# A hybrid encoder on one core: where layer two's projections find their operands inside 256 bytes

## The chip, the core and the metric

The kernel runs on one core of one Trainium2 chip. The metric is the time of one execution on the device, in microseconds (us); the time before is a median of three runs. A stage of the kernel is named below by its stretch of the profiled execution, in us from the start of the span.

## The reference

Two layers of a bidirectional encoder trunk run over 272 positions (256 tokens and 16 meta tokens) of width 2048. Everything is float32. Cut to what matters here:

```python
def _layer(h, w_in, ..., w_out, ln1_w, ln1_b, w_ff1, w_ff2, ln2_w, ln2_b):
    proj = jnp.einsum('bld,dp->blp', h, w_in)          # 2048 -> 6176 columns
    gq, gk, gv, gr, glr, nq, nk, nv = jnp.split(proj, points, axis=-1)
    y_gla = _gla_mixer(gq, gk, gv, gr, glr, ...)       # gated linear attention, 4 heads
    y_na = _na_mixer(nq, nk, nv, na_rel_bias)          # neighbourhood attention, 16 heads
    mix = jnp.einsum('blm,md->bld', jnp.concatenate([y_gla, y_na], axis=-1), w_out)
    h = _layer_norm(DEEPNORM_ALPHA * h + mix, ln1_w, ln1_b)
    ff = jnp.einsum('blf,fd->bld', jnp.square(jax.nn.relu(jnp.einsum('bld,df->blf', h, w_ff1))), w_ff2)
    return _layer_norm(DEEPNORM_ALPHA * h + ff, ln2_w, ln2_b)
...
return h[:, N_META:]                                   # the meta tokens are dropped
```

## The kernel before

The residual stream lies transposed: 16 chunks of 128 features on the partitions, positions along the free axis. Each chunk is held as two parts of type fp32r, a high part (the value as the engine rounds it) and a low part (what is left). Weights come from memory in tiles `raw` of 128 x 1024 float32 (512 KB); ScalarE makes the high part `wh` of a tile (line 152) and VectorE the low part `wl` (line 153). A product is then three products, high by high, high weight by low part, low weight by high part. Which matmuls do them depends on the number of positions:

- `three`, with n of 272, 274 or 258 columns: three matmuls, at lines 165, 166 and 167. They stream the high part, the low part and the high part again. This is called a triple below. The two columns over 272 or 256 carry a gain and a bias of the norm through the product.
- `three`, with n = 256: a matmul of 512 columns at line 161 that streams both parts in one go, and one of 256 at line 162. This is called a pair below.
- `by_k`, where a stage starts on chunks that are still being made: matmuls one by one at line 191.

`by_m` calls `three` for 16 chunks in turn and 4 output tiles; a tile of weights serves 8 chunks. Between the tiles `pump` lets other work in: the attention heads' own matmuls (lines 505 to 540 and 597 to 653) with their steps on the other engines.

Where in SBUF an operand starts is set by two tables. Each table is indexed by a stage:

```python
ROOM = 640
WIDE = (23, 276), (3, 288), (20, T)        # chunk: start of the first part, step to the second, in elements
STARTS = (40, 48), (0, 8), (36, 4)         # weights: start of wh and of wl within their tiles
...
return self.parts(t, *WIDE[(2 if name != "x" else 1) if (self.l if late is None else late) else 0])
...
yield w[t], first.pop(0) if first else 1, l + (l and j > 11)    # which row of STARTS a tile of weights takes
```

A chunk's tile has 640 elements (2560 bytes) and a tile of weights 1088 (4352 bytes), both multiples of 256 bytes, and in the built program all of them start at 64 modulo 256. The columns of a weights tile that one matmul takes start at multiples of 512 bytes from the tile's start. So modulo 256 bytes all matmuls of a stage find their operands at the same places, four bytes to an element:

| stage | chunk's parts | weights `wh`, `wl` | matmuls |
|---|---|---|---|
| layer one | 156 and 236 | 224 and 0 | triples of 272, and of 274 in its first two feed-forward groups |
| layer two's projections (row 1 of both tables) | 76 and 204 | 64 and 96 | triples of 274 (K) and 272 (V, NA's k and v), `by_k` of 272 (V), pairs (q, gate, NA's q), whose 512 columns are 256 at 76 and 256 at 204 |
| layer two's first two feed-forward groups (row 1 of `WIDE`, row 2 of `STARTS`) | 76 and 204 | 208 and 80 | triples of 258 |
| the rest of layer two (row 2 of both) | both at 144, joined, so that 512 columns are contiguous | 208 and 80 | pairs, `by_k` of 256 |

`ln_add` writes layer two's chunks where row 1 of `WIDE` puts them. When the first norm of layer two is done, `renew` writes them once more at row 2.

The program is written out in a fixed order, each engine runs its own list, and only waits for operands tie the lists together.

Of the kernel before, what the change touches and what calls it, by code (L numbers as in the profile page):

```python
# [17 lines left out]
T = 256  # L18
# [18 lines left out]


ROOM = 640
WIDE = (23, 276), (3, 288), (20, T)  # L40
STARTS = (40, 48), (0, 8), (36, 4)


class Pair(tuple):
# [7 lines left out]
class Trunk:  # L52
# [88 lines left out]
    def made(self, ap, parts, l):  # L141
        if ap is None:
# [4 lines left out]
        wh, wl = (self.wp.tile([P, WB + 64], F32R, name=nm, tag=nm)[:, at:at + size]  # L147
                  for nm, at in zip(("wh", "wl"), STARTS[l]))
        for p in range(parts):
# [72 lines left out]
    def pair(self, pool, name, c, late=None):  # L222
        if name == "sp":
            return Pair(pool.tile([P, 2, L], F32R, name=f"{name}{c}", tag=f"{name}{c}", bufs=1))
        t = pool.tile([P, ROOM], F32R, name=f"{name}{c}", tag=f"{name}{c}", bufs=1)
        return self.parts(t, *WIDE[(2 if name != "x" else 1) if (self.l if late is None else late) else 0])

# [643 lines left out]
    def renew(self, end):  # L871
# [3 lines left out]
        for c in range(f["new"], end):  # L875
            while f["ready"] <= c:
                self.step(self.bg, 1)
            if n == T:
                self.x[c] = self.parts(self.x[c].tile, *WIDE[2])
            h, lo = self.x[c]  # L880
# [140 lines left out]
```

## Time and profile before

| | |
|---|---|
| median of 3 runs | 2371.94 us (2371.65 to 2372.04) |
| profiled execution | 2372.29 us, of which the span is 2370.1 us |
| granted TensorE clock, mean | 0.997 |
| TensorE matmul (PE) busy | 2337.7 us, 99% of the span, 17276 instructions |
| TensorE weight load (PEld) busy | 2223.8 us, 94% |
| VectorE (DVE), ScalarE (ACT), GpSimd (POOL) busy | 1576.1, 1188.2 and 283.5 us |
| layer two's projections | 1212.5 to 1557.9 us |
| layer two's first two feed-forward groups | 1650.0 to 1696.6 us |

Matmuls overlap, so that the duration of one (some 0.28 us for 272 columns) says little; what the stage pays for each is the time from one start to the next, and that is read from rows in order of time or from the number of matmuls in a stretch. In a stretch, a matmul that reaches in from before or is cut off at the end counts as well, so the count is some 2 too high.

### The profile page before, as it was taken

To read this page: it belongs to the slowest core of one execution; us is meant where nothing else is said; L and a number is where in the kernel's file an instruction comes from. 1 tells how busy PE (TensorE), PEld (TensorE's weight loads), DVE (VectorE), ACT (ScalarE), POOL (GpSimd) and SP (SyncE) were. 2 spreads that over 40 slices of the span, in tenths; PEclk is the share of its full clock that TensorE was granted. 3 is DMA by queue.
4 is the path that set the end of the run, shared out by engine and by line. 5 is a ranking of instruction groups with operands and counts; after the bars stand their busy time and mean duration, and the time that the engine had idled before them with its cause. 6 is when DMAs were issued, how large, how long until landed. Compare 5 with 4: busy or idle time off the path is not lost.

```text
span 2370.1 us, 43078 instructions
## 1 busy us (share of the span) xinstructions
PE 2337.7 (99%) x17276; PEld 2223.8 (94%) x17276; DVE 1576.1 (66%) x2473; ACT 1188.2 (50%) x1962; POOL 283.5 (12%) x447
## 2 busy tenths in 40 slices
PE   9999999999999999999999999999999999999997
PEld 9999999999999999999999899998988888888886
DVE  6688787785544455557577887778866555666655
ACT  6555555564433344444456555555654334444443
POOL 1164320020000000000020454300200000000000
PEclk9999999999999999999999999999999999999998
DMA  7544444555555555545545445446565555555553
GB/s 249 169 139 150 142 141 159 177 178 181 178 179 179 182 181 178 179 182 176 181 169 194 144 151 159 139 152 204 185 191 195 194 195 194 190 195 195 190 194 132
DMA packets 118359, 417.46 MB, mean 176 GB/s; under 512 B 13388, under 2 KB 16332, under 8 KB 118160
## 3 DMA queue, kind: packets, MB, share of 16 engines
q1 hardware_dynamic: 118160, 414.72, 53.1%
q8 instruction: 135, 2.21, 0.4%
q14 instruction: 64, 0.52, 0.1%
HBM read 412.57 MB, written 2.10 MB: 175 GB/s over the span
## 4 chain that ended last, share of the span: by engine, by line
PE 91%; DVE 4%; POOL 2%; issue 1%; ACT 1%; DMA 0%; SPq 0%; ACTq 0%; POOLq 0%; DVEq 0%
PE mm L161 21%; PE mm L165 16%; PE mm L166 16%; PE mm L167 16%; PE mm L162 11%; PE mm L191 6%; POOL lev L475 1%; PE bg L505 1%; DVE wl L153 1%; PE bg L648 1%; DVE acc L864 1%; PE bg L597 1%; DVE lev L481 0%; ACT wh L152 0%; ACT ns L580 0%
## 5 line engine op out<-in xcount | busy, mean ns | idle before, releaser
L153 DVE TENSOR_TENSOR wl<-raw,wh 128x1024 fp32r<-128x1024 f32 (+1 forms) x772 | 946.0, 1226 | 617.4 <-ACT wh L152 609.2
L152 ACT CAST wh<-raw 128x1024 fp32r<-128x1024 f32 (+1 forms) x772 | 804.3, 1042 | 901.8 <-PE mm L166 351.8
L165 PE MATMUL mm<-x,wh 128*128 128x272 f32 (+2 forms) x2176 | 623.3, 286 | 0.0
L166 PE MATMUL mm<-x,wh 128*128 128x272 f32 (+2 forms) x2176 | 617.7, 284 | 0.0
L167 PE MATMUL mm<-x,wl 128*128 128x272 f32 (+2 forms) x2176 | 616.7, 283 | 0.1
L165 PEld LDWEIGHTS mm<-x,wh 128*128 128x128 f32 x2176 | 407.7, 187 | 1.2 <-issue 0.4
L166 PEld LDWEIGHTS mm<-x,wh 128*128 128x128 f32 x2176 | 408.7, 188 | 0.0
L167 PEld LDWEIGHTS mm<-x,wl 128*128 128x128 f32 x2176 | 407.6, 187 | 0.5 <-DVE wl L153 0.5
L161 PE MATMUL mm<-x,wh 128*128 128x512 f32 x1152 | 398.0, 391 | 0.0
L162 PE MATMUL mm<-x,wl 128*128 128x256 f32 x1152 | 317.9, 276 | 0.2 <-DVE wl L153 0.2
L161 PEld LDWEIGHTS mm<-x,wh 128*128 128x128 f32 x1152 | 216.2, 188 | 45.3 <-issue 0.4
L161 PE MATMUL mm<-y,wh 128*128 128x512 f32 x704 | 241.6, 388 | 0.0
L162 PEld LDWEIGHTS mm<-x,wl 128*128 128x128 f32 x1152 | 216.2, 188 | 0.7 <-DVE wl L153 0.6
L166 PE MATMUL mm<-y,wh 128*128 128x272 f32 x704 | 199.2, 283 | 0.0
L165 PE MATMUL mm<-y,wh 128*128 128x272 f32 x704 | 199.2, 283 | 0.0
L167 PE MATMUL mm<-y,wl 128*128 128x272 f32 x704 | 198.9, 283 | 0.0
L162 PE MATMUL mm<-y,wl 128*128 128x256 f32 x704 | 193.5, 275 | 0.7 <-DVE wl L153 0.7
L161 PE MATMUL mm<-u,wh 128*128 128x512 f32 x512 | 175.6, 388 | 0.0
L475 POOL TENSOR_TENSOR lev<-be 128x128 f32<-128x128 f32 (+1 forms) x256 | 150.2, 617 | 115.2 <-PE bg L505 36.4
L161 PEld LDWEIGHTS mm<-y,wh 128*128 128x128 f32 x704 | 132.0, 188 | 27.0 <-ACT wh L152 0.2
L165 PE MATMUL mm<-u,wh 128*128 128x272 f32 x512 | 144.9, 283 | 0.0
L166 PE MATMUL mm<-u,wh 128*128 128x272 f32 x512 | 144.9, 283 | 0.0
(235 smaller groups left out, 3312.5 us busy)
## 6 DMA issues: line engine op xcount, KB each, us to landing
raw<-in_wff SPq DMA_DIRECT2D x512, 512.0 KB, 3.5
raw<-in_win SPq DMA_DIRECT2D x190, 512.0 KB, 3.5
raw<-in_wout SPq DMA_DIRECT2D x64, 512.0 KB, 3.6
nb<-in_nab SPq DMA_DIRECT2D x16, 352.0 KB, 3.8
out<-acc SPq DMA_DIRECT2D x8, 256.0 KB, 2.2
xraw<-in_xT SPq DMA_DIRECT2D x7, 272.0 KB, 5.4
wraw<-in_wup SPq DMA_DIRECT2D x2, 392.0 KB
raw<-in_win SPq DMA_DIRECT2D x4, 128.0 KB, 2.9
```

What stands on the lines that cost most here:

```text
L152: nc.scalar.copy(wh[:, c], raw[:, c])
L153: self.wl = nc.vector.tensor_tensor(wl[:, c], raw[:, c], wh[:, c].bitcast(F32), ALU.subtract).ins
L161: mm(ps, lhsT=wh[:, c:c + P], rhs=x.joined, start=first, stop=False)
L162: mm(ps[:, T:], lhsT=wl[:, c:c + P], rhs=xh[:, :T], start=False, stop=last)
L165: mm(o, lhsT=wh[:, c:c + P], rhs=xh[:, :n], start=first, stop=False)
L166: mm(o, lhsT=wh[:, c:c + P], rhs=xl[:, :n], start=False, stop=False)
L167: mm(o, lhsT=wl[:, c:c + P], rhs=xh[:, :n], start=False, stop=last)
L191: self.nc.tensor.matmul(ps[m][:, :n], lhsT=parts[p][0][:, c:c + P], rhs=acts[j][parts[p][1]][:, :n], start=j + p == 0, stop=j == nk - 1 an ...
L475: tt = lambda o, x, y: nc.gpsimd.tensor_tensor(o, x, y, ALU.subtract)
L505: nc.tensor.matmul(ps[:, b], lhsT=k[:, b], rhs=q[:, r], start=True, stop=True)
L597: nc.tensor.matmul(ps[hh][:, t * NKEY:t * NKEY + NKEY], lhsT=q[hs, NM + t * P:NM + t * P + P], rhs=k[hs, t, :], start=True, stop=True)
L648: nc.tensor.matmul(r[hs], lhsT=(v2 if rest else v1)[:, t, hs], rhs=p2[:, t, :] if rest else p1[:, 2 * t + hh, :], start=rest, stop=not rest)
```

## The change

One pair of numbers in each table. Layer two's chunks, as projections read them, start 8 elements into their tile with 300 elements from part to part, in place of 3 and 288: that is 96 and 16 modulo 256 bytes in place of 76 and 204. The weights of the projections start at elements 36 and 4, as those of the rest of layer two already do: 208 and 80 in place of 64 and 96. The triples of 258 in the first two feed-forward groups read the same chunks, so that their parts move too; their weights stay at 208 and 80.

```diff
 ROOM = 640
-WIDE = (23, 276), (3, 288), (20, T)
-STARTS = (40, 48), (0, 8), (36, 4)
+WIDE = (23, 276), (8, 300), (20, T)
+STARTS = (40, 48), (36, 4), (36, 4)
```

Every engine's list has the same instructions in the same order before and after, with the same waits; only addresses differ.

## The prediction

> **What bounds the kernel now.** First the page's busy times and the chain that ended last:
>
> ```profile
> PE 2337.7 (99%) x17276; PEld 2223.8 (94%) x17276; DVE 1576.1 (66%) x2473; ACT 1188.2 (50%) x1962; POOL 283.5 (12%) x447
> PE 91%; DVE 4%; POOL 2%; issue 1%; ACT 1%; DMA 0%; SPq 0%; ACTq 0%; POOLq 0%; DVEq 0%
> ```
>
> TensorE is busy all the time and carries 91% of the chain. Then the busy times by stretch, for the stages whose addresses change. The columns are the stretch, its length, and busy us with the instruction count for PE, PEld, DVE, ACT and POOL; then the granted clock, the DMA share and GB/s. The rows are layer two's projections as a whole, among them the gate's stretch, and the two feed-forward groups with 258 columns.
>
> ```profile
> 1212.50:1557.90 345.40, 339.15 (x2494) 315.23 (x2492) 277.89 (x489) 210.10 (x432) 130.12 (x205) 1.00 0.48 158
> 1315.90:1380.60 64.70, 61.36 (x371) 53.52 (x369) 58.30 (x94) 40.40 (x82) 41.64 (x70) 1.00 0.42 144
> 1650.00:1696.60 46.60, 46.60 (x391) 46.58 (x390) 43.54 (x76) 34.57 (x63) 13.12 (x8) 1.00 0.54 182
> ```
>
> PE idles 6.3 of 345.4 us in the projections, 3.3 of them in the gate's stretch, and not at all with 258 columns. The granted clock is 1.00. So a nanosecond per matmul, gained or lost, reaches the end nearly whole. The matmuls affected are counted from groups within the projections (the triples are also on lines 166 and 167, and the pairs' second matmul is on line 162):
>
> ```profile
> L161 PE MATMUL mm<-x,wh 128*128 128x512 f32 x320 | 115.0, 399 | 0.0
> L165 PE MATMUL mm<-x,wh 128*128 128x272 f32 x320 | 93.4, 292 | 0.0
> L167 PE MATMUL mm<-x,wl 128*128 128x274 f32 x64 | 18.5, 289 | 0.1
> L191 PE MATMUL mm<-x,wh 128*128 128x272 f32 x128 | 20.2, 287 | 0.1
> ```
>
> That is 320 pairs, 320 triples of 272, 64 triples of 274, and by the code 192 single matmuls at line 191 (these 128 and half as many on `wl`). To them come 2 x 64 = 128 triples of 258.
>
> **What a placement costs today.** Nothing is added or removed; the whole change is the time from one matmul's start to the next. The rows for that, by placement. First stretches of the same matmul throughout: layer one's triples of 272; line 191 on 272 in layer two; the pairs on contiguous parts.
>
> ```profile
> 600.00:1000.00 400.00, 400.00 (x3275) 400.00 (x3274) 203.40 (x225) 164.74 (x209) 0.00 (x0) 1.00 0.56 180
> 1244.50:1258.50 14.00, 14.00 (x115) 14.00 (x115) 11.27 (x19) 6.45 (x8) 0.90 (x2) 1.00 0.70 231
> 1740.00:2230.00 490.00, 490.00 (x2884) 433.83 (x2883) 294.24 (x377) 218.46 (x283) 0.00 (x0) 1.00 0.59 194
> ```
>
> Less the some 2 cut off at the edges (3 with the longer 512s) these are 122.2 ns a matmul, 124.2 ns, and 340.1 ns a pair. Then rows in order of time (start, duration, engine, line), the first and last of undisturbed series: 24 pairs, 11 triples of 272, 31 of 274, 64 of 258.
>
> ```profile
> 1263.09 0.39 PE L161 MATMUL mm<-x,wh 128*128 128x512 f32 x1
> ...
> 1271.07 0.39 PE L161 MATMUL mm<-x,wh 128*128 128x512 f32 x1
> ```
> ```profile
> 1532.29 0.28 PE L165 MATMUL mm<-x,wh 128*128 128x272 f32 x1
> ...
> 1535.99 0.28 PE L165 MATMUL mm<-x,wh 128*128 128x272 f32 x1
> ```
> ```profile
> 1219.00 0.29 PE L165 MATMUL mm<-x,wh 128*128 128x274 f32 x1
> ...
> 1230.21 0.28 PE L165 MATMUL mm<-x,wh 128*128 128x274 f32 x1
> ```
> ```profile
> 1656.26 0.28 PE L165 MATMUL mm<-x,wh 128*128 128x258 f32 x1
> ...
> 1678.94 0.28 PE L165 MATMUL mm<-x,wh 128*128 128x258 f32 x1
> ```
>
> Divided by 23, 10, 30 and 63: a pair takes 347.0 ns, a triple of 272 takes 370.0, of 274 takes 373.7, of 258 takes 360.0.
>
> Columns alone don't explain this: 272 against 258 is 5% more columns and 3% more time. What does fit is the number of 16-byte blocks (four columns) that a stream touches. The contiguous pair starts on a multiple of 16 (144) and touches 128 + 64 = 192 blocks: 340.1 / 192 = 1.771 ns a block. Layer one's parts start 12 bytes past a multiple of 16 (156, 236), so 272 columns touch 69 blocks: 122.2 / 69 = 1.771 ns. Two stages, the same quotient. I take it as the floor, and what a row has above it as its excess, in ns:
>
> - triple of 272 at 76/204, also 12 past: 3 x 69 blocks, floor 366.6, excess 3.4;
> - triple of 274: 3 x 70, floor 371.9, excess 1.8;
> - pair, two 256s and one more: 3 x 65, floor 345.3, excess 1.7;
> - line 191 on 272: floor 122.2, excess 2.0;
> - triple of 258: 3 x 66, floor 350.6, excess 9.4. These are split parts beside weights at 208 and 80, which is what the projections are to get;
> - contiguous parts beside weights at 208 and 80: excess 0.
>
> [...]
>
> **The change part by part.**
>
> *The chunk's parts.* 96 and 16 are multiples of 16, so each stream loses one block: 272 columns touch 68, 274 touch 69, 256 touch 64, 258 touch 65. The new floors are 361.3, 366.6, 340.0 (pair), 120.4 (line 191) and 345.3. Against today's times that is, with no excess left: 320 x 8.7 + 64 x 7.1 + 320 x 7.0 + 192 x 3.8 + 128 x 14.7 ns = 2.8 + 0.5 + 2.2 + 0.7 + 1.9 = 8.1 us less. That is the lower end.
>
> *The weights and how they meet the parts.* The excess at the new places isn't in the trace. Written as e ns for each triple or pair and e/3 for a single matmul, it adds (320 + 64 + 320 + 128 + 64) x e = 0.896 us for each ns of e. One bound is e = 0, the contiguous pairs' with the same weights. From the other side, the slowest series with these weights are a few pairs early in layer two's output projection:
>
> ```profile
> 1604.24 0.40 PE L161 MATMUL mm<-y,wh 128*128 128x512 f32 x1
> ...
> 1605.31 0.39 PE L161 MATMUL mm<-y,wh 128*128 128x512 f32 x1
> ...
> 1606.33 0.39 PE L161 MATMUL mm<-y,wh 128*128 128x512 f32 x1
> ```
>
> Three pairs take 357 ns each, within the rows' rounding of 10 ns in 1070, and the next three 340, at the same addresses: up to 17 above the floor, or some 8 a matmul. Between these ends I take e = 9.4, the excess of the 258s. It is the only row where these weights meet split parts. Then the sum is -8.1 + 0.896 x 9.4 = +0.3 us. By parts: triples of 272 go from 370.0 to 370.7 (+0.2 us), of 274 from 373.7 to 376.0 (+0.2), pairs from 347.0 to 349.4 (+0.8), line 191 from 124.2 to 123.5 (-0.1), and 258s from 360.0 to 354.7 (-0.7).
>
> *Making the weights.* A tile's two halves were made at three placements; here layer two's projections (64/96) and the rest of layer two (208/80), with count, busy us and mean ns:
>
> ```profile
> L153 DVE TENSOR_TENSOR wl<-raw,wh 128x1024 fp32r<-128x1024 f32 x16 | 19.6, 1224 | 11.0 <-ACT wh L152 10.8
> L152 ACT CAST wh<-raw 128x1024 fp32r<-128x1024 f32 x17 | 17.8, 1047 | 14.5 <-PE mm L166 7.9 <-DMA raw<-in_win 3.5 <-issue 1.3
> L153 DVE TENSOR_TENSOR wl<-raw,wh 128x1024 fp32r<-128x1024 f32 x181 | 221.8, 1225 | 183.6 <-ACT wh L152 181.7
> L152 ACT CAST wh<-raw 128x1024 fp32r<-128x1024 f32 x180 | 188.9, 1050 | 272.1 <-PE mm L161 165.2 <-issue 106.9
> ```
>
> 1224 and 1225 ns, 1047 and 1050: the writes don't feel the address. They also have cover, since a tile serves 8 x 347 ns = 2.8 us of pairs. If it were gone, 3 ns on each of some 100 tiles would be 0.3 us. I cost it, and the chunks' own writes, at nothing. Waits stay as they are.
>
> *Sum.* +0.3 us on the profiled execution's 2372.29 (span 2370.1 and 2.2 around it), which lies 0.35 above the median of the runs. On the median, that is 2372.3.
>
> **The rivals.**
>
> *Faster: the excess nearly vanishes.* For it: the contiguous pairs have none beside these very weights, and all new starts are multiples of 16. Against it: every split placement in layer two has some. The times today hint at where it would stop: 340.0, 346.7, 360.0, 366.7 and 373.3 are 51, 52, 54, 55 and 56 steps of 6.67 ns, and all rows but the 370.0 of the 272s lie on them. Were the new times the next step above their floors, the triples of 272 would go to 366.7 (-1.1 us), of 274 to 366.7 (-0.4), pairs to 340.0 (-2.2), 258s to 346.7 (-1.7) and line 191 to 122.2 (-0.4): -5.8 us, 2366.1. With no excess at all it is -8.1 us, 2363.8. [...]
>
> *Slower: parts and weights collide at every matmul.* The series at 357 ns shows that these weights can cost some 7 to 8 ns a matmul even beside parts on a multiple of 16. With 7: triples and pairs of 832 groups get 512 x 21 + 320 x 14 ns, line 191 gets 192 x 7, together 16.6 us, less the 8.1 of the blocks: +8.5 us, 2380.4. It decides from e = 14.4 on (+4.8 us). Against it: there the series was short and followed a disturbance; in the quiet stages after it, 340 holds. For it: in the projections the attention's own matmuls break in every few us, so series there seldom settle, and 76/204 beside 64/96 stays within 3.4 ns of its floor, which leaves more to lose than to win in the weights' part.
>
> *Hidden.* In the gate's stretch PE waits 3.3 us for the attention heads' steps, so a gain or loss on its 128 pairs (at most 0.9 us of the 8.1) could go into that wait. It changes no sign and gets no chance of its own.
>
> **How the numbers follow.** Excess like the 258s', within 4.7 us of now: 0.43. The collision: 0.32. The vanishing excess: 0.25. A measurement of this kernel tells 0.2% (4.7 us) from no change; the three cases fall one to each verdict, so faster 0.25, same 0.43, slower 0.32. The predicted time is the likeliest's, 2372.3. The range reaches to the stepped result of the faster rival and most of the way into the slower one: 2365.8 to 2379.0. The likeliest alone would lie between 2368 and 2376.
>
> **What would show it.** Starts in the changed kernel: pairs at 349 ns, triples of 272 at 371, of 274 at 376, of 258 at 355 if the sum is right. 340, 361 to 367, 367 and 345 to 347 are the faster rival; 354 and 382 the slower. Layer one's 122.2, the later pairs' 340.1 and the two halves' 1225 and 1050 ns must stand as they are; if the later pairs settle at another speed, upstream timing reaches past its stage and all of this is wrong.

## The result, and the profile after

The changed kernel takes 2375.24 us (median of 21 runs, 2373.89 to 2376.95) against 2371.94 before (21 runs, 2370.99 to 2372.92): 3.3 us more. The ratio is 1.0013, 95% interval 1.0007 to 1.0019. It is slower, clear of the interval, and within the 0.2% called no change. Its runs lie in two clusters, 2373.9 to 2374.8 (10 runs) and 2375.2 to 2377 (11), and the median is the lowest run of the upper one, so that its last half microsecond hangs on a run or two. The profiled execution (2373.98 us, span 2371.9) is of the lower one, so that its trace explains 1.7 to 2 us of the 3.3.

The stages that answer to those shown of before, each from its first matmul to its last: layer two's projections, the gate's stretch in them, and the two feed-forward groups of 258 columns. Columns as before.

```profile
1212.50:1559.70 347.20, 341.54 (x2494) 317.78 (x2492) 277.76 (x489) 210.20 (x432) 129.11 (x204) 1.00 0.51 157
1316.75:1381.50 64.75, 61.56 (x371) 53.53 (x369) 58.37 (x95) 40.41 (x82) 41.51 (x70) 1.00 0.46 145
1651.80:1698.50 46.70, 46.70 (x392) 46.70 (x391) 43.71 (x77) 34.73 (x63) 13.11 (x8) 1.00 0.61 182
```

The projections take 347.2 us in place of 345.4, the gate's stretch 64.8 in place of 64.7, and the 258s what they took. PE's busy time grew by more, 341.5 us against 339.2, and its idle time fell from 6.3 to 5.7 us: no new waits, but matmuls that follow each other more slowly, and waits that hide some of it. Series in order of time, first and last rows: 24 pairs, 32 triples of 274, 16 of 272, 7 of 272 that start 13 us after them, 54 of 258.

```profile
1263.52 0.40 PE L161 MATMUL mm<-x,wh 128*128 128x512 f32 x1
...
1271.49 0.40 PE L161 MATMUL mm<-x,wh 128*128 128x512 f32 x1
```
```profile
1219.12 0.29 PE L165 MATMUL mm<-x,wh 128*128 128x274 f32 x1
...
1231.00 0.29 PE L165 MATMUL mm<-x,wh 128*128 128x274 f32 x1
```
```profile
1299.84 0.29 PE L165 MATMUL mm<-x,wh 128*128 128x272 f32 x1
...
1305.53 0.29 PE L165 MATMUL mm<-x,wh 128*128 128x272 f32 x1
...
1312.97 0.28 PE L165 MATMUL mm<-x,wh 128*128 128x272 f32 x1
...
1315.17 0.28 PE L165 MATMUL mm<-x,wh 128*128 128x272 f32 x1
```
```profile
1662.73 0.28 PE L165 MATMUL mm<-x,wh 128*128 128x258 f32 x1
...
1681.81 0.28 PE L165 MATMUL mm<-x,wh 128*128 128x258 f32 x1
```

A pair takes 346.5 ns here (before 347.0), a triple of 274 takes 383.2 (373.7), a triple of 272 first 379.3 and then 366.7 at the same addresses (370.0), a triple of 258 still 360.0. Line 191's 272s, layer one's 272s and the later pairs, from stretches:

```profile
1245.00:1259.00 14.00, 14.00 (x114) 14.00 (x114) 10.89 (x17) 6.41 (x8) 0.89 (x2) 1.00 0.68 218
600.00:1000.00 400.00, 400.00 (x3275) 400.00 (x3274) 203.29 (x225) 164.63 (x209) 0.00 (x0) 1.00 0.59 181
1740.00:2230.00 490.00, 490.00 (x2883) 433.74 (x2882) 293.53 (x375) 217.83 (x282) 0.00 (x0) 1.00 0.64 194
```

Line 191 goes to some 125 ns (112 matmuls in 14 us); from start to start its undisturbed steps grew from 123.5 to 125.4 ns. What the change doesn't touch stands at 122.2 and 340.1.

### The profile page after: what moved, and what is told of

It reads as the page before. It is cut to its first block, busy times and chain, and to the rows that moved or that the text cites. A ratio compares the mean times of both kernels' runs of the same rounds, so it can differ in the third digit from the quotient of the medians.

```text
span 2371.9 us, 43078 instructions
## 1 busy us (share of the span) xinstructions
PE 2340.2 (99%) x17276; PEld 2226.9 (94%) x17276; DVE 1575.8 (66%) x2473; ACT 1187.7 (50%) x1962; POOL 282.0 (12%) x447
## 4 chain that ended last, share of the span: by engine, by line
PE 92%; DVE 3%; POOL 2%; issue 1%; ACT 1%; DMA 0%; SPq 0%; ACTq 0%; POOLq 0%; DVEq 0%
PE mm L161 22%; PE mm L165 16%; PE mm L166 16%; PE mm L167 16%; PE mm L162 11%; PE mm L191 6%; POOL lev L475 1%; PE bg L505 1%; DVE wl L153 1%; PE bg L648 1%; DVE acc L864 1%; PE bg L597 1%; DVE lev L481 0%; ACT wh L152 0%; PE bg L337 0%
```

## The experiments

Three theories were written down before the runs. A: the weights' new place costs, the parts' start on a multiple of 16 gains. B: the parts cost, whatever the weights. C: neither by itself, only how parts and weights meet. The expectations of the two halves and of the two places taken from a map name them so.

**One half of the change alone.** `e1_parts_only`:

```diff
-WIDE = (23, 276), (3, 288), (20, T)
+WIDE = (23, 276), (8, 300), (20, T)
```

> Only the parts move (96 and 16), the projections' weights stay at 64 and 96; 258s as in the changed kernel. Theory A, the weights' place at 208 and 80 makes the loss and the parts' starts on a multiple of 16 make a gain: faster than before, by 2 to 8 us (2364 to 2370), triples of 272 at 361 to 367 ns. Theory B, the loss comes from the parts alone, whatever the weights: like the changed kernel, 2374 to 2376, triples of 274 near 383 ns. Theory C, neither by itself but how the two meet: within 2 us of before, or anywhere; triples then differ from both kernels.

`e2_weights_only`:

```diff
-STARTS = (40, 48), (0, 8), (36, 4)
+STARTS = (40, 48), (36, 4), (36, 4)
```

> Only the projections' weights move (208 and 80), the parts stay at 76 and 204. Theory A: slower than the changed kernel's 2375, by the blocks that aren't saved, up to 2380; triples of 272 near 380 ns. Theory B: like before, 2371 to 2373, triples of 272 at 370 ns and of 274 at 374. Theory C: not the sum of the two halves of the change with e1.

The parts alone took 2374.73 us against 2371.91 (ratio 1.0012, 1.0003 to 1.0021), the weights alone 2374.29 (1.0009, 1.0000 to 1.0018). Each half costs 2.4 to 2.8 us and both together 3.3: by the medians they don't add up, though the intervals are wide, and A's gain isn't there. By kinds of matmul it is plainer. Means over all undisturbed series of each trace, worked out from the starts, in ns:

| kernel | parts, weights | 272 | 274 | pair | 258 |
|---|---|---|---|---|---|
| before | 76/204, 64/96 | 370.5 | 373.6 | 347.4 | 360.0 |
| parts alone | 96/16, 64/96 | 373.9 | 385.8 | 350.9 | 360.0 |
| weights alone | 76/204, 208/80 | 379.7 | 373.4 | 348.6 | 353.5 |
| changed | 96/16, 208/80 | 375.7 | 382.9 | 348.4 | 359.9 |

The new weights make the 272s dear beside the old parts (+9.2) and hardly dearer beside the new (+1.8). For 274s it is the parts that matter. A falls with the time of the parts alone, where it wanted a gain of 2 to 8 us, and B with the 272s of the weights alone, which it wanted at 370. C is what is left; its own expectation of the time (within 2 us, or anywhere) was too loose to be tested here. (The 258s of the weights-alone kernel have the very addresses of before's. More on them below.)

**The same distances at another place.** `e3_both_64_on` moves both by 64 bytes:

```diff
+WIDE = (23, 276), (24, 300), (20, T)
+STARTS = (40, 48), (52, 20), (36, 4)
```

> The changed kernel with the parts and the projections' weights both 64 bytes further (160 and 80; 272, that is 16, and 144), so that the distances stay. If only the distance of a stream from the weights counts, the projections' matmuls take what they take in the changed kernel (274s 383 ns, 272s 376, pairs 348) and the time is within 1 us of 2375, but for the 258s, whose weights don't move with them. If the place in 256 bytes itself counts, the triples change by several ns.

2375.0 us against 2371.91 (1.0012, 1.0003 to 1.0021), 272s 374.5, 274s 381.0, pairs 348.4: within 2 ns of the changed kernel for each. That agrees with a law of distances. It doesn't prove one, since series of this kind scatter by more than 2 ns (379.3 and 366.7 at the same addresses in the changed kernel).

**A map of quiet series.** `m1_map` computes nothing of the layers:

```python
for k in range(16):
    matmul(ps[:, :n], lhsT=w[wh + k % 8 * P], rhs=x[:, xh:xh + n])     # high by high
    matmul(ps[:, :n], lhsT=w[wh + k % 8 * P], rhs=x[:, xl:xl + n])
    matmul(ps[:, :n], lhsT=w[wl + k % 8 * P], rhs=x[:, xh:xh + n])     # or a pair in their place
```

> Nothing of the layers is computed: a kernel of matmul series alone, 149 placements, each with 16 triples or pairs on one PSUM bank, run in one order and then in the reverse one; starts are read from the trace. Blocks theory: with both parts at the same start a and weights at 208 and 80, a of 0, 16, 32, 48 take 3 x 1.77 = 5.3 ns less a triple of 272 than the other twelve starts, 361.3 against 366.6, if the excess is the same. Steps theory: all quiet series lie on multiples of 6.67 ns, so 366.7 for both. For the kernels' placements: before 370 (272), 374 (274), 347 (pair); after 376, 383, 348; a rival, that the differences come from the work around the series and not from the placement, gives the same time for both in these quiet series.

Without any surrounding work, the kernels' placements gave, in the two orders: before 369.9 and 370.0 (272s), 380.0 and 373.4 (274s); changed 366.6 and 376.6, 383.4 twice; weights alone 380.0 twice, 373.4 twice; parts alone 373.2 and 373.4, 386.6 twice. These are close to the kernels' own numbers. So the placement makes them, and the rival, that the surroundings alone do, falls. With both parts at one start a and weights at 208/80, 272s took 380.0, 375.8, 377.1 and 373.2 ns at a of 0, 16, 32 and 48, against 370.0 at 44 and 373.4 at 12 and 28: no 5.3 ns for the multiples of 16 over those 12 past one. But 4 past a multiple was dear, 380 to 387 ns at 4, 20, 36 and 52. Most times are multiples of 3.33 ns, as 366.6, 370.0, 373.4, 376.6, 380.0, 383.4 and 386.6 are here within 0.1.

`m2_map`, the same with 344 placements in two random orders:

> Nothing of the layers is computed: series alone again, 344 of them in two different random orders, so that each placement has other series ahead of it. Each of the kernels' placements stands 5 times, 10 runs of each. If a placement fixes its time, all 10 agree within 0.5 ns; if a series can settle in several ways, some placements show two or more times a step of 3.3 or 6.7 ns apart: before's 272s one time only (its runs lie within 2 us), the changed kernel's several (366.6 and 376.6 were seen). Contiguous pairs, start swept by 4 bytes: the blocks theory wants 340 on the four multiples of 16 and 345 to 347 on the other twelve; that only the meeting with the weights counts, no such pattern. 170 random placements for 272s, four-byte starts: if 361.3 is a floor that can be reached, some lie under 366; if 55 steps of 6.67 is the least, none.

Before's 272s took 370.0 in all 10 runs. The changed kernel's took 366.6 to 366.8 in six, 376.6 to 376.8 in three and 380.0 in one. Layer one's placement took 366.6 to 366.8 in all 10, parts alone 373.3 to 373.6 in 10, weights alone 380.0 in 10. Before's 274s took 373.3 in seven and 380.0 in three. The rows below are two series at the changed kernel's addresses and one at before's: first and last of 16 triples each.

```profile
127.01 0.28 PE L1383 MATMUL aur<-x,wh 128*128 128x272 f32 x1
...
132.52 0.28 PE L1383 MATMUL aur<-x,wh 128*128 128x272 f32 x1
```
```profile
3235.55 0.29 PE L1383 MATMUL auq<-x,wh 128*128 128x272 f32 x1
...
3241.20 0.29 PE L1383 MATMUL auq<-x,wh 128*128 128x272 f32 x1
```
```profile
322.25 0.28 PE L1383 MATMUL cbr<-x,wh 128*128 128x272 f32 x1
...
327.80 0.28 PE L1383 MATMUL cbr<-x,wh 128*128 128x272 f32 x1
```

Over 15 steps these are 367.3, 376.7 and 370.0 ns (a series' first steps can differ from the rest: the pairs at a start of 16, further down, begin with two steps of some 350 and go on at 340.0). One placement, two speeds, each held to the end: the changed kernel's 379 and 367 above are most likely the same thing. What picks the speed is not shown. Different series ran ahead of the two, but that can't be all of it: a series of before's, further down, changes its speed with the same program ahead of it.

Of 170 random placements for 272s, none was under 366.6, the median took 379.9 and the slowest 400.0. And the contiguous pairs, start swept, weights at 208/80: 16 took 340.0, but 0 took 344.5, 32 took 349.2, 48 took 346.6 and 350.0, while 28, not a multiple of 16, took 343.3. The last row pairs, a start of 36 (356.7 over the series) and one of 16 (341.3, settled at 340.0):

```profile
1330.39 0.40 PE L1387 MATMUL ipr<-x,wh 128*128 128x512 f32 x1
...
1335.74 0.40 PE L1387 MATMUL ipr<-x,wh 128*128 128x512 f32 x1
```
```profile
203.46 0.39 PE L1387 MATMUL bhr<-x,wh 128*128 128x512 f32 x1
...
208.58 0.39 PE L1387 MATMUL bhr<-x,wh 128*128 128x512 f32 x1
```

With the start held at 144 and both weights swept in steps of 32, contiguous pairs took 346 to 354 ns, never the 340.0 of 208/80. The weights' place matters even where the stream starts on a multiple of 16.

The second map does show a pattern within 16 bytes, but it isn't the blocks'. The times are means over the last ten steps of each series, in ns. Of the random placements, whose weights are random too, the table takes those whose two parts start alike:

| start past a multiple of 16, bytes | blocks of 272 columns | random 272s: placements | mean and range | swept contiguous pairs |
|---|---|---|---|---|
| 0 | 68 | 9 | 374.8, 366.6 to 380.0 | 340 to 350 |
| 4 | 69 | 19 | 384.7, 380.0 to 393.4 | 350 to 360 |
| 8 | 69 | 10 | 379.1, 373.3 to 385.5 | 350 to 367 |
| 12 | 69 | 13 | 372.4, 370.0 to 376.4 | 343 to 347 |

Starts 12 past are as good as multiples of 16 or better, and 4 past costs 10 to 12 ns a triple more than these two. A count of blocks gives 4, 8 and 12 the same time. On average, then, the change moved the parts from the best of these four places, 76 and 204, to the second best. Why they differ so, no run shows.

**Two places taken from the map.** `e4_as_layer_one`, the best known:

```diff
+WIDE = (23, 276), (23, 276), (20, T)
+STARTS = (40, 48), (40, 48), (36, 4)
```

> Layer two's projections at layer one's places: parts at 156 and 236, weights at 224 and 0 (the 258s keep weights at 208 and 80). The first map's quiet series give triples of 272 367, of 274 373, pairs 347 there. Theory C (how parts and weights meet decides, and the map carries over to the kernel): 272s at 367 in place of before's 370.5, so 320 x 3.5 = 1.1 us, plus up to 0.5 us at line 191, less than before: 2370 to 2371. A rival, that what surrounds the series decides more than the place: 272s scatter over 367 to 380 as in the changed kernel, 2373 to 2376.

272s 367.4, 274s 373.9, pairs 347.6, 258s 354.9. The median is 2371.39 us against 2371.69 (ratio 0.9998, 0.9989 to 1.0007): a shade lower, not to be told from before, and 0.4 us above the 2370 to 2371 expected. The 272s came out as the map had them. `e9_bad_place`, a slow one:

```diff
+WIDE = (23, 276), (45, 293), (20, T)
+STARTS = (40, 48), (20, 21), (36, 4)
```

> A place that the second map shows to be slow: parts at 244 and 136, weights at 144 and 148, where a quiet triple of 272 took 388.1 ns in both orders. Theory C, the map carries over: the kernel's 272s settle at 388, 17.6 ns above before's 370.5, so 320 x 17.6 = 5.6 us, and with line 191's 192 matmuls at a third of that (1.1 us) about 2378 to 2379; the 274s, pairs and 258s at these places weren't in the map and can move it by some 2 us either way. The rival, that the surrounding work decides: 272s at 370 to 376, 2372 to 2376.

2381.58 us against 2371.98 (ratio 1.0041, 1.0028 to 1.0055): 9.6 us more, and some 3 us above the 2378 to 2379 expected. A series of its triples of 272, the first and the last of 15:

```profile
1301.68 0.29 PE L165 MATMUL mm<-x,wh 128*128 128x272 f32 x1
...
1307.07 0.29 PE L165 MATMUL mm<-x,wh 128*128 128x272 f32 x1
```

That is 385.0 ns over 14 steps. Means are 385.6 (272s; some 388 in the map), 386.7 (274s), 355.6 (pairs), 363.5 (258s). Now the differences to before times the counts, with line 191's stretch from its length in the trace. The last two columns are the medians' difference and, from the same execution as the paces, the span's difference to before's 2370.1:

| kernel | 272 x 320 | 274 x 64 | pair x 320 | line 191 | 258 x 128 | sum, us | measured, us | same execution, us |
|---|---|---|---|---|---|---|---|---|
| changed | 1.7 | 0.6 | 0.3 | 0.3 | 0.0 | 2.8 | 3.3 | 1.8 |
| parts alone | 1.1 | 0.8 | 1.1 | 0.1 | 0.0 | 3.1 | 2.8 | 2.3 |
| weights alone | 2.9 | 0.0 | 0.4 | 0.3 | -0.8 | 2.7 | 2.4 | 1.8 |
| both 64 on | 1.3 | 0.5 | 0.3 | 0.3 | 0.0 | 2.3 | 3.1 | 3.5 |
| as layer one | -1.0 | 0.0 | 0.1 | 0.1 | -0.7 | -1.4 | -0.3 | -0.5 |
| bad place | 4.8 | 0.8 | 2.6 | 0.8 | 0.4 | 9.6 | 9.6 | 8.4 |

Six placements, and the sum holds within 1.2 us for each, by either column. In the same execution it is 0.8 to 1.2 us too far from zero for five: it counts every matmul at the undisturbed pace, and waits take up a part. In the changed kernel PE's busy time grew by 2.4 us in the projections and their length by 1.8. Both 64 on is 1.2 us too low, which the waits and the clock below account for. The -0.8 for the 258s of the weights alone is no gain of placement, since their addresses are before's. So the matmuls' own pace is what the change costs in this execution; what the upper cluster adds is another matter.

**What scatters the runs.** `e5_changed_again`, `e6_changed_again`, `e7_changed_again` are the changed kernel as it is, `e8_before_again` the kernel before:

> The changed kernel as it is, for another profile: its runs lie in two clusters, near 2374 and near 2376, and the profile at hand is of the lower (2373.98). If the upper one is the gate stretch's wait for the attention heads (in e3's profile, 2375.89, the wait before line 505 at 1342 us is 2.2 us in place of 0.8 and the granted clock 0.93 after it), a profile at 2375.5 or above shows a long wait there and 66 to 67 us for the stretch, and one near 2374 a short wait and 64.8. If the upper cluster is triples that settle at 377 to 380 rather than at 367, the triples' stretches are longer and the wait short.

> The changed kernel once more, for one more profile: at 2375.5 or above a long wait and 66 to 67 us in the gate's stretch, near 2374 a short one and 64.8.

> The changed kernel once more, for one more profile: at 2375.5 or above a long wait and 66 to 67 us in the gate's stretch, near 2374 a short one and 64.8.

> The kernel before as it is, for another profile. Its runs lie within 2371 to 2373. By either reading it shows what its first profile did: triples of 272 at 370.5, the wait at 1342 us about 1 us or less, 64.7 us for the gate's stretch.

All three came out in the lower cluster (2373.93, 2374.14 and 2373.83 us), with 64.8 us in the gate's stretch, so they don't show what the upper one is. The kernel with both 64 on was profiled at a time like the upper cluster's (2375.89 us). There GpSimd's steps of an attention head take longer, in order of time from the changed kernel's profile and from `e3_both_64_on`'s: GpSimd's steps (start, duration, how many rows are merged), and the matmuls that wait for what is made of them.

```profile
1331.64 5.51 POOL L475 TENSOR_TENSOR lev<-be 128x128 f32<-128x128 f32 x8 [0.38 <-PE bg L505]
...
1343.94 0.68 PE L505 MATMUL bg<-lev 128*128 128x128 f32 x4 [0.78 <-DVE lev L481]
```
```profile
1331.77 6.63 POOL L475 TENSOR_TENSOR lev<-be 128x128 f32<-128x128 f32 x8 [0.44 <-PE bg L505]
...
1345.19 0.68 PE L505 MATMUL bg<-lev 128*128 128x128 f32 x4 [2.19 <-DVE lev L481]
```

And the stretch from 1340 to 1365 by busy times and clock (the third number from the end), the changed kernel first; of `e3_both_64_on` also the 6 us behind the wait:

```profile
1340.00:1365.00 25.00, 24.22 (x141) 21.17 (x140) 21.58 (x32) 16.07 (x33) 12.41 (x19) 1.00 0.52 165
```
```profile
1340.00:1365.00 25.00, 22.81 (x125) 19.86 (x124) 20.57 (x30) 15.16 (x30) 13.24 (x21) 0.93 0.45 147
1345.00:1347.00 2.00, 1.81 (x9) 1.66 (x10) 0.27 (x2) 0.92 (x3) 1.05 (x1) 0.78 0.47 188
1347.00:1349.00 2.00, 2.00 (x8) 1.65 (x7) 2.00 (x4) 1.56 (x4) 1.87 (x2) 0.50 0.03 8
1349.00:1351.00 2.00, 2.00 (x11) 1.79 (x10) 2.00 (x3) 0.00 (x0) 2.00 (x4) 0.86 0.35 66
```

Eight steps take 6.63 us in place of 5.51, PE waits 2.19 us in place of 0.78, and right behind that wait the granted clock falls to 0.50 for a few microseconds, which costs some 1.7 us (what the three stretches of 2 us lack to 1.00). This gate's stretch is 67.0 us long in place of 64.8. The parts alone waited 2.1 us here and the bad place 2.0, with GpSimd's eight steps at 6.63 and 6.50 us, and kept a clock of 1.00 from 1340 to 1365; the parts alone took 65.7 us for the stretch. So such a wait cost about 1 us in the parts alone, and the clock fell behind it in one profile of three, which cost more. What makes GpSimd's steps longer isn't shown: in the kernel with the weights alone they start 0.3 us later than here and take 5.51 us.

The changed kernel's runs have their mean granted clock beside them: 0.997 in all 13 up to 2375.71 us, and 0.996 in 7 of the 8 from 2376.08 us on, the value of the profile above. It is 0.996 in the 4 slowest runs of the parts alone and the 6 slowest of both 64 on as well, and in none of before's runs that list it. So these runs lost clock too, which triples that merely settle slower would not explain. In which stretch they lost it isn't shown.

The second profile of before brought something else. Its 258s, 58 triples:

```profile
1657.81 0.28 PE L165 MATMUL mm<-x,wh 128*128 128x258 f32 x1
...
1677.95 0.28 PE L165 MATMUL mm<-x,wh 128*128 128x258 f32 x1
```

That is 353.3 ns, where the first profile of the same kernel had 360.0. The same series of the same program settles one step of 6.67 ns apart from one execution to the next. The second map had 353.3 for this placement in 10 of 10 runs, so even that didn't tell of the 360.0. For the 128 triples the step is some 0.8 us. Which of the two before's other runs took isn't known; against the faster one the changed kernel's 258s cost some 0.8 us as well.

## Why the prediction was right or wrong, point by point

- *No change that a measurement tells (0.43).* It came so by the 0.2% that the prediction set: +3.3 us, 0.14%. The 21 runs do tell it from nothing, with 1.0007 as the lower end of the interval. The time lies in the range and in the likeliest case's own range (2368 to 2376), above the 2372.3 forecast. The 0.3 us of the sum was ten times too small, and that the time still came so near is luck: two terms of 8 us each, neither of which the runs bear out, stood against each other in the sum.
- *A gain or a loss per matmul reaches the end nearly whole.* Right in the main, but not so whole: PE's busy time in the projections grew by 2.4 us, its idle time shrank by 0.6, and 1.8 us reached the end of that execution. The case called hidden, with 0.9 us in the gate's stretch, pointed the right way, though little of it was there (idle 3.3 to 3.2 us).
- *A floor of 1.771 ns for each 16-byte block, 8.1 us to be had from aligned starts.* Wrong, and the step that failed. In the maps, 272s at multiples of 16 and all other starts end at the same 366.6 at best, never near the 361.3, and contiguous pairs at four starts on multiples of 16 took 340 to 350. Two quotients that agreed at two well-placed stages were not a law. By the maps there is no price for each block touched: random 272s whose parts both start 12 past a multiple of 16, with 69 blocks, took 372.4 ns on average, and those on a multiple, with 68, took 374.8. The place within 16 bytes does matter, since 4 past took 384.7 with 69 blocks as well.
- *An excess of 9.4 ns for split parts beside weights at 208 and 80.* Mis-sized, and taken for what it isn't. Above its block floors the changed kernel has 14.4 (272s), 16.3 (274s), 8.4 (pairs) and 14.6 ns (258s). And before's 9.4 was one of two beats of one series; its second profile and the quiet series of the second map had 2.7. Summed by the counts, with 4.6 for line 191, the excess comes to 11.1 us in place of 8.4, and less the 8.1 of the blocks that is +3.0 in place of +0.3.
- *258s from 360.0 to 354.7.* Wrong: 359.9, and 360.0 in all 10 quiet series of the second map. The 360.0 they started from wasn't a fixed pace of before's either. *274s to 376.0, 272s to 370.7:* too low by 7 and 5 ns. *Pairs to 349.4:* 348.4. *Line 191 from 124.2 to 123.5:* 125.4. The 124.2 was misread: 115 matmuls less 2 in 14 us are 123.9, and the starts give 123.5. A saving of 8.1 us that wasn't there, and a cost of 8.4 us on top of it where the paces of all these matmuls together rose by 2.8 us, were errors in opposite directions and largely met.
- *Steps of 6.67 ns* were given to the faster rival. They are real, in halves, 3.33 ns: 312 of the 400 series of 272s in the second map lie within 0.35 ns of a multiple of it. Had the sum gone to the next step above each floor it would still have been a gain; which step a placement takes is not read from block counts.
- *No excess at all, -8.1 us, the far end of the faster rival.* It would have the weights' new place cost nothing. With only the weights moved, quiet triples of 272 go from 370.0 to 380.0 in 10 runs of 10.
- *Making the weights costs nothing.* Right: 1224 and 1047 ns in the changed kernel's projections, as before.

```profile
L153 DVE TENSOR_TENSOR wl<-raw,wh 128x1024 fp32r<-128x1024 f32 x16 | 19.6, 1224 | 10.3 <-ACT wh L152 10.0
L152 ACT CAST wh<-raw 128x1024 fp32r<-128x1024 f32 x17 | 17.7, 1047 | 13.6 <-PE mm L166 8.3 <-DMA raw<-in_win 2.1 <-issue 1.2
```

## What to carry to other kernels

Here TensorE was busy back to back with fp32r matmuls, and the place of stream and weights within 256 bytes moved its pace by several per cent: 366.6 to 400.0 ns for a triple of 272. No count of blocks read from a profile gave the pace here; a kernel of quiet series, many placements in one run, gave it for the triples of 272 within some 3 ns, except where a placement has several paces. Paces from a kernel's own trace, times the counts, gave the whole kernel's time within 1.2 us; the map's alone missed the bad place by some 3 us, mostly because it had only the triples of 272 there. Run each placement several times behind different series: one that always settles at the same step is worth more than one that is sometimes faster, and a good place found this way (layer one's) may leave nothing more to win.

## What the runs showed that was not expected

- One series of matmuls at fixed addresses settles at one of several paces, 3.33 to some 13 ns apart, and mostly keeps it, as 58 triples of 258 in a row kept 353.3: 366.7, 376.7 or 380.0 for the changed kernel's 272s, 353.3 or 360.0 for before's 258s in two executions of one program.
- The weights, a tile of their own, move the pace of a stream by their start alone: 370.0 or 380.0 ns for a triple, and 340.0 or 346 to 354 for contiguous pairs.
- The stream's place within 16 bytes shows on average, and not in the order of blocks touched: 372.4 ns for random triples of 272 with both parts 12 bytes past a multiple of 16, 374.8 on one, 379.1 at 8 past, 384.7 at 4 past.
- A wait of 2.2 us on TensorE was followed by a granted clock of 0.50 for a few microseconds in one profile, where waits of 2.1 and 2.0 us at the same place left it at 1.00 in two others.
